# A two-block transformer-like kernel: later convolution tiles, FFNs that open on three outputs, and an earlier second half of a values' projection

## The chip, the cores and the metric

The kernel runs on one core of one Trainium2 chip. The metric is the device time of one execution in microseconds (us); lower is better. The core has TensorE (PE, matrix products into PSUM; its weight loads are listed as PEld), VectorE (DVE), ScalarE (ACT), GpSimd (POOL) and SyncE (SP), which issues the DMAs. Each engine executes its own list of instructions in order.

## The reference

All data are float32, with 512 tokens and a width of 1024. The first block is a hybrid layer: a gated causal depthwise convolution of 31 taps over 1024 channels, a state-space recurrence (S5) over 32 groups with 64 complex states, gates and an output projection. The second block is a stack of two layers, each with two SwiGLU feed-forward networks (FFNs) around a mixer; the first mixer is a short convolution beside an RWKV recurrence, the second a latent attention with 8 heads.

```python
# first block
proj = rms_norm(x) @ w_in                     # ca, cb, z_c, u_s, z_s, g_c, g_s
cu = causal_depthwise_conv(ca * sigmoid(cb))  # 31 taps
cu = silu(layer_norm(cu))
conv_out = (cu * silu(z_c)) @ w_conv_out
y = gelu(s5(u_s)); y = y * sigmoid(y @ w_glu + b_glu)
ssm_out = (y * silu(z_s)) @ w_ssm_out
x = x + rms_norm((sigmoid(g_c) * conv_out + sigmoid(g_s) * ssm_out) @ w_out)
# second block, for layer 0 (even mixer) and layer 1 (odd mixer, attention)
x = x + 0.5 * swiglu(rmsnorm(x)); x = x + mixer(rmsnorm(x)); x = x + 0.5 * swiglu(rmsnorm(x))
```

## The kernel before

**Layout and products.** The activations lie transposed, channels on partitions and 512 tokens along the row, in 8 tiles of 128 channels (`P.x`). A float32 product is made of three products in a reduced format (`mm3`, L248 to L250): the high part of the weights with the high and the low part of the data, and the low part of the weights with the high part of the data. `wload` (L235 to L237) brings 1024 weight columns by a DMA from SP into `raw` (2 buffers), casts them on ACT to `wh` and makes the remainder `wl` on DVE, each of them in 3 buffers. A projection of two outputs (`proj`) is 48 products of 128x128 by 128x512 and needs two such loads.

**Order.** The program is traced in the order of the code. A planner then makes each engine's list: it goes by priority (normally the order of the code), by free buffers and by times that it estimates itself. `tc.issue_after(ins)` keeps what is traced in its block behind `ins` on the same engine. Buffers of one tag are given out in turn.

**First block.** `block1` follows two hand-written orders, `ORDER_A` and `ORDER_B`. A letter is a step, a digit its number. `p` and `P` are projections whose gated product feeds the convolution: `p` (0, 3, 5, 7) leaves a tile `cu`, `P` (1, 2, 4, 6) leaves split tiles `cph`/`cpl`. `t` (`toeplitz`, L730 on) convolves channels of a `P` tile on PE with 96 products of 256 columns and four weight loads. `c` (`conv_`) convolves channels of a `p` tile with 31 instructions: tiles 0 and 3 on POOL (L765, with ACT's products), tiles 5 and 7 on DVE (L767, L770). Class `c` has its priority lowered by 20000, so that it fills gaps. `u` projects the S5 inputs and writes them to DRAM, `s` and `z` project gates (`zs`, `zc`). `T` makes S5's tables (L366 to L490, mainly DVE), `R` the rotation tables (`s5_rot`, L507 to L512, one chain of DVE instructions). `Q` and `K` are the two halves of `s5_pre` for a quarter of the groups (POOL outer products; then PE transposes and products and 16 small DMAs). `q`, `r`, `x`, `w` are the four parts of `s5_main` for a quarter: input products (L583), rotation and scan (L588 to L594), rotation back (L597 to L603), output products (L608, L609). `q`, `r`, `x`, `w` and `K` are kept behind the last PE product that was traced before them (`P.last_mm`). The convolution tiles on POOL are kept behind `P.last_gp` and those on DVE behind `P.last_dve`; `P.last_dve` is set in `s5_rot` (L512). In `ORDER_B`, `y` and `G` finish the S5 branch, `g` projects the output gates, `L` is the layer norm over all eight convolution tiles (it begins with L847 on `sacc`, the sum that POOL makes at L778 and L780), `S` and `C` are the two output projections. The output tiles of `z` lie in pools that are opened after those of S5 are closed.

**FFN.** `ffn` runs four times. Each of two halves makes 11 pairs (gate, up), each pair from one load of 2048 columns, and then 8 outputs of the down projection. The first FFN gets `cols=HALVES` and opens otherwise: gate 0, up 0 and gate 1 are made together, tile of data by tile of data, so that each new tile of data feeds three outputs. The other three begin with all of gate 0, then up 0. Inputs `xh`, `xl` come tile by tile from the stage before (L270, L271). The banks of PSUM are given out anew at each stage.

**Odd mixer.** `odd` makes key parts for all heads (`kall`), half of the values (`vproj(0)`, 24 products, L1889 to L1891, with evacuations L1893 and L1894), then keys and queries for pairs of heads (`kpair`, `qpair`). `kpair` reads rows of `nd` back from DRAM as broadcasts, multiplies (L1828) and splits. `qpair` makes 27 products, a rotation (L1755 on the result of L1855) and row sums (L1869). The second half of the values, `vproj(1)`, comes after the second pair's keys and queries, in two banks.

Of the kernel before, what the change touches and what calls it, by code (L numbers as in the profile page):

```python
# [296 lines left out]
def ffn(P, L, j, nxt, out=None, cols=()):  # L297
# [4 lines left out]
    with tc.tile_pool(name=f"f{L}{j}", bufs=2) as ph, tc.tile_pool(name=f"m{L}{j}", bufs=1) as mp:  # L302
# [4 lines left out]
        first = []  # L307
        if cols:
            w0, w1 = P.wload(gu[0], 2048), P.wload(gu[1], 1024)
            pss = [P.ps() for _ in range(4)]  # L310
            for s in cols:
                for k in range(8):
                    for ps, (h, l), o in ((pss[0], w0, 0), (pss[1], w0, 1024), (pss[2], w1, 0)):
                        P.mm3(ps[:, s], h, l, o + 128 * k, [P.xh[k][:, s]], [P.xl[k][:, s]], k == 0, k == 7)
            h, l = P.wload(gu[1][:, 1024:], 1024)
            P.mm3(pss[3], h, l, 0, P.xh, P.xl)
            first = [pss[0:2], pss[2:4]]
# [176 lines left out]
def s5_rot(P, tb):  # L494
# [5 lines left out]
    for i in range(6):  # L500
        m = 1 << i
        n = min(32, 512 // m)
        for g0 in range(0, 32, n):
            g = slice(g0, g0 + n)
            cq, sq = (a[:, g].unsqueeze(2).to_broadcast([128, n, m]) for a in tb["rot"][i])
            A, B = (x[:, 0:n * m].rearrange("p (g k) -> p g k", g=n) for x in (ta, tb_))
            V.tensor_tensor(out=A, in0=c[:, g, 0:m], in1=cq, op=ALU.mult)  # L507
            V.tensor_tensor(out=B, in0=s[:, g, 0:m], in1=sq, op=ALU.mult)
            V.tensor_tensor(out=c[:, g, m:2 * m], in0=A, in1=B, op=ALU.subtract)
            V.tensor_tensor(out=A, in0=s[:, g, 0:m], in1=cq, op=ALU.mult)  # L510
            V.tensor_tensor(out=B, in0=c[:, g, 0:m], in1=sq, op=ALU.mult)
            P.last_dve = V.tensor_tensor(out=s[:, g, m:2 * m], in0=A, in1=B, op=ALU.add)  # L512
# [50 lines left out]
def s5_main(P, tb, q, u_dram, y_dram):  # L563
# [39 lines left out]
    V.tensor_tensor(out=sh[:, :, 1:64], in0=st3[:, :, 0:63], in1=vr3[:, :, 0:63], op=ALU.subtract)  # L603
# [354 lines left out]
def proj_first(P, src, xT, sqx):  # L958
# [33 lines left out]
    for a in range(2):  # L992
# [6 lines left out]
ORDER_A = ("p0 P1 p3 t1 u0 u1 T Q0 P2 R0 K0 t2 Q1 c0 q0 K1 s0 r0 P4 x0 q1 Q2 s1 w0 r1 K2 p5 c3 x1 q2 Q3 t4 w1 r2 K3 P6 c5 "  # L999
           "x2 q3 t6 w2 r3 p7 x3 w3 c7")  # L1000
ORDER_B = "z0 z1 z2 z3 y0 g0 g1 g2 y1 y2 y3 g3 G L g4 g5 g6 S0 g7 S1 C0 C1 C2 C3 C4 C5 C6 C7"
# [652 lines left out]
def odd(P, nxt):  # L1654
# [14 lines left out]
    with ExitStack() as ctx:  # L1669
# [304 lines left out]

        K, Q = kpair(0), qpair(0, "all")
        for p in range(4):
# [4 lines left out]
            if p == 0:  # L1981
                vproj(1, "mm")
                S.put(*kvh, *kvl)
# [54 lines left out]
```

## Time and profile before

| | us |
|---|---|
| median of three runs | 2653.73 |
| lowest and highest run | 2647.78, 2653.99 |
| the profiled execution, own time | 2650.77 |
| span of the profiled execution | 2649.0 |
| PE busy | 2512.6 |
| DVE busy | 1474.5 |
| ACT busy | 925.5 |
| POOL busy | 484.2 |

The span runs from the first to the last instruction; the execution's own time is 1.8 us longer. PE is busy for 95% of the span, and the work that PE has to do is the same in each version of an order, so the difference between span and busy time, 136.4 us, is what an order can win, besides time in which PE ran at the lower of its two clocks. The profile gives the granted clock as a share of full speed (1.00 is 2.4 GHz, 0.50 is 1.2 GHz). By time the stages are: first block to about 576 us, first FFN to 937, even mixer to 1319, second FFN to 1680, third to 2040, odd mixer to 2278, last FFN to the end.

### The profile page before, as it was taken

How to read it: one execution, taken by the hardware profiler on the slowest of the kernel's cores; microseconds unless marked ns; L12 is line 12 of the kernel's file. 1: busy time of each engine (PE TensorE's matmuls, PEld its weight loads, DVE VectorE, ACT ScalarE, POOL GpSimd, SP SyncE). 2: the span in 40 equal slices, each digit the busy share in tenths (PEclk: the TensorE clock that was granted, in tenths of full speed). 3: DMA queues.
4: the chain of work that ended last, by engine and by line, in shares of the span. 5: the costliest groups of instructions: out<-in, count | busy, mean ns of one | idle time of the engine just before them, and what ended most of it. 6: DMA issues, size and time to landing. Idle time of an engine off the chain costs nothing.

```text
span 2649.0 us, 31923 instructions
## 1 busy us (share of the span) xinstructions
PE 2512.6 (95%) x12724; PEld 2052.6 (77%) x12724; DVE 1474.5 (56%) x1978; ACT 925.5 (35%) x1322; POOL 484.2 (18%) x332
## 2 busy tenths in 40 slices
PE   8687899999999998999899999999999889999999
PEld 7566788878888876787588888888888677788887
DVE  7888868455344469643754344543444766543443
ACT  5253436243222333222332233322223565422221
POOL 2499602020000164331100000100001231100000
PEclk9798899999999998998999999999999989999999
DMA  5222332313232332314132322322324412222323
GB/s 169 80 85 75 92 111 89 127 66 110 87 105 99 113 129 59 74 49 132 41 100 88 107 96 90 102 98 92 105 86 138 113 62 72 70 97 85 106 93 98
DMA packets 116294, 250.94 MB, mean 95 GB/s; under 512 B 44112, under 2 KB 53072, under 8 KB 116144
## 3 DMA queue, kind: packets, MB, share of 16 engines
q1 hardware_dynamic: 116000, 248.68, 29.7%
q8 instruction: 100, 1.64, 0.3%
q14 instruction: 50, 0.41, 0.0%
q10 hardware_dynamic: 144, 0.22, 0.0%
HBM read 234.30 MB, written 13.37 MB: 93 GB/s over the span
## 4 chain that ended last, share of the span: by engine, by line
PE 78%; DVE 9%; POOL 3%; issue 2%; DMA 2%; ACT 2%; SPq 0%; DVEq 0%; ACTq 0%; POOLq 0%
PE bank L248 24%; PE bank L249 24%; PE bank L250 24%; POOL xa L765 1%; DVE wl L237 1%; DMA s<-nd 1%; PE bank L1913 1%; DVE xa L770 1%; PE bank L1270 1%; POOL acc L265 1%; PE bank L1333 0%; ACT wh L236 0%; PE bank L1346 0%; DVE xl L271 0%; PE bank L1406 0%
## 5 line engine op out<-in xcount | busy, mean ns | idle before, releaser
L248 PE MATMUL bank<-xh,wh 128*128 128x512 f32 (+1 forms) x2152 | 836.7, 391 | 13.6 <-ACT xh L977 5.8
L236 ACT CAST wh<-raw 128x1024 fp32r<-128x1024 f32 x448 | 433.3, 968 | 1187.2 <-PE bank L249 852.5
L249 PE MATMUL bank<-xl,wh 128*128 128x512 f32 (+1 forms) x2152 | 838.0, 390 | 4.3 <-DVE xl L947 2.7
L250 PE MATMUL bank<-xh,wl 128*128 128x512 f32 (+1 forms) x2152 | 836.3, 389 | 2.7 <-DVE wl L237 2.7
L237 DVE TENSOR_TENSOR wl<-raw,wh 128x1024 fp32r<-128x1024 f32 (+2 forms) x414 | 482.7, 1166 | 331.8 <-ACT wh L236 329.3
L248 PEld LDWEIGHTS bank<-xh,wh 128*128 128x128 f32 x2152 | 406.8, 190 | 103.1 <-ACT xh L977 6.5
L249 PEld LDWEIGHTS bank<-xl,wh 128*128 128x128 f32 x2152 | 407.9, 190 | 92.1 <-DVE xl L978 4.6
L250 PEld LDWEIGHTS bank<-xh,wl 128*128 128x128 f32 x2152 | 407.8, 189 | 87.7 <-DVE wl L237 3.6
L265 POOL TENSOR_TENSOR acc<-acc,sq 128x512 f32<-128x512 f32 x54 | 90.1, 1669 | 1298.2 <-ACT sq L264 1291.6
L249 PE MATMUL bank<-ml,wh 128*128 128x512 f32 x704 | 273.9, 389 | 0.0
L250 PE MATMUL bank<-mh,wl 128*128 128x512 f32 x704 | 273.9, 389 | 0.0
L248 PE MATMUL bank<-mh,wh 128*128 128x512 f32 x704 | 272.6, 389 | 0.0
L332 DVE TENSOR_TENSOR up<-bank,rs 128x512 f32<-128x512 f32 x88 | 60.8, 691 | 271.5 <-PE bank L250 271.4
L328 DVE TENSOR_TENSOR gp<-bank,rs 128x512 f32<-128x512 f32 x88 | 60.8, 691 | 174.9 <-PE bank L250 174.7
L250 PEld LDWEIGHTS bank<-mh,wl 128*128 128x128 f32 x704 | 132.2, 188 | 27.6
L249 PEld LDWEIGHTS bank<-ml,wh 128*128 128x128 f32 x704 | 132.2, 188 | 27.4
L248 PEld LDWEIGHTS bank<-mh,wh 128*128 128x128 f32 x704 | 132.2, 188 | 27.3
L237 POOL TENSOR_TENSOR wl<-raw,wh 128x1024 fp32r<-128x1024 f32 x34 | 82.9, 2440 | 139.7 <-ACT wh L236 112.7
L765 POOL TENSOR_TENSOR xa<-xa,cw 128x512 f32<-128x512 f32 x60 | 98.0, 1635 | 10.7 <-ACT cw L764 8.1
L340 DVE SCALAR_TENSOR_TENSOR xa<-bank,xa 128x512 f32<-128x512 f32 x64 | 44.3, 692 | 79.5 <-PE bank L250 79.5
L254 ACT CAST mh<-m 128x512 fp32r<-128x512 f32 x88 | 55.1, 626 | 58.5 <-DVE m L334 58.5
L743 PE MATMUL bank<-cph,wh 128*128 128x256 f32 x128 | 41.0, 320 | 32.2 <-ACT cph L726 32.2
(654 smaller groups left out, 2927.8 us busy)
## 6 DMA issues: line engine op xcount, KB each, us to landing
raw<-in_ffn_gu_dram SPq DMA_DIRECT2D x176, 512.0 KB, 3.5
raw<-in_ffn_dn_dram SPq DMA_DIRECT2D x64, 512.0 KB, 3.5
raw<-in_w_in_dram SPq DMA_DIRECT2D x46, 512.0 KB, 3.5
raw<-in_even_in_dram SPq DMA_DIRECT2D x26, 512.0 KB, 3.5
raw<-in_ffn_dn_dram SPq DMA_DIRECT2D x64, 192.0 KB, 2.3
raw<-in_conv_dram SPq DMA_DIRECT2D x16, 512.0 KB, 3.8
xa<-in_xT_dram SPq DMA_DIRECT2D x16, 256.0 KB, 4.1
raw<-in_w_co_dram SPq DMA_DIRECT2D x8, 512.0 KB, 3.3
```

Of the source, the lines that this page charges most:

```text
L236: nc.scalar.copy(h[:, :m], raw[:, :m])
L237: self.wlo.tensor_tensor(out=l[:, :m], in0=raw[:, :m], in1=h[:, :m].bitcast(F32), op=ALU.subtract)
L248: self.nc.tensor.matmul(ps, h[i][:, s], xh[k], start=a, stop=False)
L249: self.nc.tensor.matmul(ps, h[i][:, s], xl[k], start=False, stop=False)
L250: last = self.nc.tensor.matmul(ps, l[i][:, s], xh[k], start=False, stop=b)
L254: self.nc.scalar.copy(hi, src)
L265: nc.gpsimd.tensor_tensor(out=acc, in0=acc, in1=sq, op=ALU.add)
L328: nc.vector.tensor_tensor(out=gp, in0=pg, in1=rs, op=ALU.mult)
L332: nc.vector.tensor_tensor(out=up, in0=pu, in1=rs, op=ALU.mult)
L340: nc.vector.scalar_tensor_tensor(out=P.x[o], in0=ps, scalar=0.5, in1=P.x[o], op0=ALU.mult, op1=ALU.add)
L743: nc.tensor.matmul(d, h[:, o], xh, start=a, stop=False)
L765: GP.tensor_tensor(out=y, in0=y, in1=w, op=ALU.add)
```

## The change

The change has three parts. In `ffn` the opening on three outputs becomes the only one; the three FFNs that had the plain opening take it with whole rows (`slice(0, T)`). In the first block `ORDER_A` is rearranged: step `P2` comes ahead of `u0`, `s0` ahead of `K0`, `P4`, `t4`, `s1`, `P6`, `t6` and `p7` each move forward by one place or more; `c5` and `c7` leave `ORDER_A` and stand behind `z0` in `ORDER_B`; `P.last_dve` is now the last DVE instruction of a step `x` (L603), so that both DVE convolution tiles stay behind step `x3`. In `odd`, `vproj(1)` stands ahead of the first pair's keys and queries and takes its banks from the large group.

```diff
--- before.py
+++ after.py
@@ -294,7 +294,7 @@
 HALVES = (slice(0, 256), slice(256, 512))
 
 
-def ffn(P, L, j, nxt, out=None, cols=()):
+def ffn(P, L, j, nxt, out=None, cols=(slice(0, T),)):
     nc, tc = P.nc, P.tc
     gu, dn = P.ap["ffn_gu"][L * 2 + j], P.ap["ffn_dn"][L * 2 + j]
     rs = P.rs
@@ -304,17 +304,15 @@
         mh = [mp.tile([128, T], R, name=f"mh{i}") for i in range(11)]
         ml = [mp.tile([128, T], R, name=f"ml{i}") for i in range(11)]
         acc = None
-        first = []
-        if cols:
-            w0, w1 = P.wload(gu[0], 2048), P.wload(gu[1], 1024)
-            pss = [P.ps() for _ in range(4)]
-            for s in cols:
-                for k in range(8):
-                    for ps, (h, l), o in ((pss[0], w0, 0), (pss[1], w0, 1024), (pss[2], w1, 0)):
-                        P.mm3(ps[:, s], h, l, o + 128 * k, [P.xh[k][:, s]], [P.xl[k][:, s]], k == 0, k == 7)
-            h, l = P.wload(gu[1][:, 1024:], 1024)
-            P.mm3(pss[3], h, l, 0, P.xh, P.xl)
-            first = [pss[0:2], pss[2:4]]
+        w0, w1 = P.wload(gu[0], 2048), P.wload(gu[1], 1024)
+        pss = [P.ps() for _ in range(4)]
+        for s in cols:
+            for k in range(8):
+                for ps, (h, l), o in ((pss[0], w0, 0), (pss[1], w0, 1024), (pss[2], w1, 0)):
+                    P.mm3(ps[:, s], h, l, o + 128 * k, [P.xh[k][:, s]], [P.xl[k][:, s]], k == 0, k == 7)
+        h, l = P.wload(gu[1][:, 1024:], 1024)
+        P.mm3(pss[3], h, l, 0, P.xh, P.xl)
+        first = [pss[0:2], pss[2:4]]
         for hh in range(2):
             for f in range(11):
                 if first:
@@ -509,7 +507,7 @@
             V.tensor_tensor(out=c[:, g, m:2 * m], in0=A, in1=B, op=ALU.subtract)
             V.tensor_tensor(out=A, in0=s[:, g, 0:m], in1=cq, op=ALU.mult)
             V.tensor_tensor(out=B, in0=c[:, g, 0:m], in1=sq, op=ALU.mult)
-            P.last_dve = V.tensor_tensor(out=s[:, g, m:2 * m], in0=A, in1=B, op=ALU.add)
+            V.tensor_tensor(out=s[:, g, m:2 * m], in0=A, in1=B, op=ALU.add)
     tb["cs"] = c, s
 
 
@@ -600,7 +598,7 @@
     st3, p23, vr3 = (a.rearrange("p (g k) -> p g k", g=8) for a in (st, p2, vr))
     V.tensor_tensor(out=vr3[:, :, 0:63], in0=p23[:, :, 0:63], in1=s[:, :, 0:63], op=ALU.mult)
     V.tensor_tensor(out=st3[:, :, 0:63], in0=st3[:, :, 0:63], in1=c[:, :, 0:63], op=ALU.mult)
-    V.tensor_tensor(out=sh[:, :, 1:64], in0=st3[:, :, 0:63], in1=vr3[:, :, 0:63], op=ALU.subtract)
+    P.last_dve = V.tensor_tensor(out=sh[:, :, 1:64], in0=st3[:, :, 0:63], in1=vr3[:, :, 0:63], op=ALU.subtract)
     yield
     py = P.side("py")
     for g in range(8):
@@ -996,9 +994,9 @@
 
 FIRST = (("w", 0, slice(0, 256)), ("x", 0, None), ("w", 0, slice(256, 1024)), ("x", 1, None), ("x", 2, None),
          ("w", 1, slice(0, 512)), ("x", 3, None), ("w", 1, slice(512, 1024)), ("x", 4, None), ("x", 5, None), ("x", 6, None), ("x", 7, None))
-ORDER_A = ("p0 P1 p3 t1 u0 u1 T Q0 P2 R0 K0 t2 Q1 c0 q0 K1 s0 r0 P4 x0 q1 Q2 s1 w0 r1 K2 p5 c3 x1 q2 Q3 t4 w1 r2 K3 P6 c5 "
-           "x2 q3 t6 w2 r3 p7 x3 w3 c7")
-ORDER_B = "z0 z1 z2 z3 y0 g0 g1 g2 y1 y2 y3 g3 G L g4 g5 g6 S0 g7 S1 C0 C1 C2 C3 C4 C5 C6 C7"
+ORDER_A = ("p0 P1 p3 t1 P2 u0 u1 T Q0 t2 R0 s0 K0 P4 Q1 c0 q0 K1 t4 r0 s1 x0 q1 Q2 p5 w0 r1 K2 P6 c3 x1 q2 Q3 t6 w1 r2 K3 p7 "
+           "x2 q3 w2 r3 x3 w3")
+ORDER_B = "z0 c5 c7 z1 z2 z3 y0 g0 g1 g2 y1 y2 y3 g3 G L g4 g5 g6 S0 g7 S1 C0 C1 C2 C3 C4 C5 C6 C7"
 B1_CLASS = {"c": "C", "t": "V", "R": "T", "T": "T", "Q": "Q", "K": "Q", "q": "S", "r": "S", "x": "S", "w": "S", "y": "S", "G": "S", "L": "L"}
 B1_PRIO = {"A": 0, "T": 0, "Q": 0, "S": 0, "C": 20000, "V": 0, "L": 0, "Z": 50000}
 CU_BUFS = 4
@@ -1972,15 +1970,14 @@
         TS(out=qe, in0=qe, scalar1=1e-6, scalar2=None, op0=ALU.mult)
         S.put(cqs)
 
+        vproj(1, "all")
+        S.put(*kvh, *kvl)
         K, Q = kpair(0), qpair(0, "all")
         for p in range(4):
             Kn = Qn = None
             if p < 3:
                 prio("N")
                 Kn, Qn = kpair(p + 1), qpair(p + 1)
-            if p == 0:
-                vproj(1, "mm")
-                S.put(*kvh, *kvl)
             if p == 2:
                 prio("O")
                 xload((4, 5, 6, 7, 0, 1, 2, 3))
```

## Rows read from the trace of the kernel before

**Rows 1.** The page's busy time by engine: share of the span, instructions.

```profile
PE 2512.6 (95%) x12724; PEld 2052.6 (77%) x12724; DVE 1474.5 (56%) x1978; ACT 925.5 (35%) x1322; POOL 484.2 (18%) x332
```

**Rows 2.** Stretches: length; busy PE, PEld, DVE, ACT, POOL; clock; DMA share, GB/s.

```profile
57.00:320.00 263.00, 203.01 (x1065) 169.57 (x1065) 217.92 (x250) 104.02 (x152) 195.96 (x134) 0.86 0.27 82
217.00:285.00 68.00, 44.65 (x247) 37.49 (x246) 67.32 (x57) 28.65 (x43) 57.78 (x35) 0.75 0.22 61
362.00:410.00 48.00, 48.00 (x213) 39.78 (x212) 20.56 (x24) 16.31 (x22) 0.00 (x0) 1.00 0.29 99
600.00:700.00 100.00, 100.00 (x441) 82.47 (x440) 52.18 (x64) 33.91 (x43) 0.00 (x0) 1.00 0.29 94
2100.00:2200.00 100.00, 75.78 (x373) 60.58 (x374) 68.79 (x153) 58.85 (x118) 33.43 (x24) 0.86 0.32 93
```

**Rows 3.** PE's waits, whole span: total us, times, longest.

```profile
PE bank L743 <- ACT cph L726: 32.2, 2, 18.6
PE bank L1755 <- ACT s L1855: 13.2, 1, 13.2
```

**Rows 4.** Timeline of PE, first block: start, length, instruction, [idle before <- releaser].

```profile
108.40 0.58 PE L743 MATMUL bank<-cph,wh 128*128 128x256 f32 x1 [18.61 <-ACT cph L726]
...
275.15 0.58 PE L743 MATMUL bank<-cph,wh 128*128 128x256 f32 x1 [13.62 <-ACT cph L726]
...
315.91 0.29 PE L609 MATMUL bank<-sh,w 128*128 128x64 f32 x1 [0.40 <-DVE sh L603]
...
409.82 0.59 PE L847 MATMUL bank<-sacc,ones 128*128 128x512 f32 x1
...
476.81 0.39 PE L248 MATMUL bank<-cah,wh 128*128 128x512 f32 x1
```

**Rows 5.** Timeline of DVE around step T, 73 to 109 us.

```profile
73.50 1.10 DVE L785 TENSOR_TENSOR u<-bank,rsl 128x512 f32<-128x512 f32 x1 [3.29 <-PE bank L250]
...
79.98 0.09 DVE L406 MEMSET pr<- 128x32 f32 x1
...
101.94 0.68 DVE L699 TENSOR_TENSOR vb<-bank,rsl 128x512 f32<-128x512 f32 x1
...
108.38 0.69 DVE L727 TENSOR_TENSOR cpl<-cp,cph 128x512 fp32r<-128x512 f32 x1 [1.43 <-ACT cph L726]
```

**Rows 6.** DVE's groups by line: two rows of 217 to 315 us, one of 315 to 362.

```profile
L770 DVE SCALAR_TENSOR_TENSOR xa<-cu,hcw,xa 128x512 f32<-128x512 f32 x30 | 39.7, 1323 | 0.6
L237 DVE TENSOR_TENSOR wl<-raw,wh 128x1024 fp32r<-128x1024 f32 x12 | 24.6, 2051 | 8.4 <-ACT wh L236 8.4
...
L770 DVE SCALAR_TENSOR_TENSOR xa<-cu,hcw,xa 128x512 f32<-128x512 f32 x30 | 22.5, 749 | 0.5
```

**Rows 7.** Timeline of POOL: its last convolution instructions, and the last sum.

```profile
303.06 4.03 POOL L765 TENSOR_TENSOR xa<-xa,cw 128x512 f32<-128x512 f32 x3
...
360.43 1.29 POOL L780 TENSOR_TENSOR sacc<-sacc,xa 128x512 f32<-128x512 f32 x1 [45.81 <-DVE xa L770]
```

**Rows 8.** Timelines of PE and ACT in the odd mixer.

```profile
2120.64 1.22 PE L1755 MATMUL bank<-s,perm 128*128 128x512 f32 x1 [13.21 <-ACT s L1855]
...
2135.09 0.80 PE L1889 MATMUL bank<-wh,s 128*128 128x512 f32 x1
...
2119.91 0.68 ACT L1855 ACTIVATE s<-bank,vec 128x512 f32<-128x512 f32 x1
...
2138.88 0.69 ACT L1893 ACTIVATE xh<-bank,scol 128x512 fp32r<-128x512 f32 x1 [1.09 <-PE bank L1891]
```

**Rows 9.** Timelines of PE and DVE where FFNs open.

```profile
2282.66 0.80 PE L248 MATMUL bank<-xh,wh 128*128 128x512 f32 x1 [3.92 <-DVE xa L1952]
...
1319.72 0.47 PE L248 MATMUL bank<-xh,wh 128*128 128x512 f32 x1 [0.56 <-DVE xa L1532]
...
592.79 0.50 PE L248 MATMUL bank<-xh,wh 128*128 128x512 f32 x1 [0.30 <-ACT wh L236]
...
2281.93 0.68 DVE L1952 TENSOR_TENSOR xa<-xa,bank 128x512 f32<-128x512 f32 x1
```

## The prediction

> **What bounds the kernel now.** I read first the page's busy times [rows 1]: PE works 2512.6 of 2649.0 us, so 136.4 us of idle PE is all that an order can give, plus what PE loses at its lower clock. A table of stretches then shows where the idle time is [rows 2]. In an FFN (600 to 700 us) PE is busy throughout, at full clock: 441 products in 100 us, 0.227 us each, which is the price of a product below. From 57 to 320 us, in the first block, PE is busy for 203.0 of 263 us, at 0.86 of full clock: 60.0 us idle. From 2100 to 2200 us, in the odd mixer, it is busy for 75.8 of 100 us. The list of PE's waits [rows 3] names the causes: 32.2 us in two waits of a toeplitz step for its `cph` tile and 13.2 us in one wait of a query's rotation; a fourth, 3.92 us, stands where the last FFN opens [rows 9]. All lie in the three places that the change touches.
>
> In the first block the timeline [rows 4] has the two toeplitz waits: t2 at 108.40 (18.61 us) and the last one, t6, at 275.15 (13.62 us). Both tiles were late on DVE, not on PE. For t2 the evacuation of P2 (L699) begins at 101.94, inside the S5 tables, although DVE had stood idle between the evacuations of u before (3.29 us ahead of the one at 73.50) [rows 5]. For t6 the place is 217 to 285 us, where DVE is busy for 67.3 of 68 us and POOL for 57.8 [rows 2]: 30 of the 31 instructions of c5 take 39.7 us there [rows 6], between S5's steps, the weights' low parts and P6.
>
> **Part 1, the first block.** I count from step u on; the PE work in it doesn't change. Step by step:
>
> - t2. P2 is now projected ahead of u, so its DVE work falls where DVE was idle, and t2 has its data when u ends. The wait of 18.61 us [rows 4] goes.
> - What that costs. P2's 48 products are 48 x 0.227 = 10.9 us by which u, and with it the S5 tables, come later: in the trace the tables start right behind the last u (79.98) [rows 5]. Part of that comes back, since P2's own DVE work, which now stands between tables and rotation chain, leaves that place. It begins with `vb` at 101.94 (0.68 us) and ends with `cpl` at 108.38 (0.69 us), which waited 1.43 us for ACT [rows 5]; table instructions stand between, so I count only P2's: `vb`, `ca` and `cpl` at 0.68 us, `cp` in four quarters at 1.7 us in all, and that wait, 5.2 us. S5 starts 10.9 - 5.2 = 5.7 us later. I charge it in full as new idle time of PE: +5.7. The bounds are 0 (s0, P4 and t4 now stand there to fill PE) and 10.9.
> - t6. Its wait followed from c5 [rows 6]. c5 leaves DVE's crowded stretch (39.7 us) and P6 moves up by a round of S5. The wait of 13.62 us goes [rows 4].
> - PE's clock. Both waits were followed by slow products: the first of t2 and of t6 took 0.58 us [rows 4]. 57 to 320 us ran at 0.86 [rows 2]. For a loss of half the speed over about 5 us after each wait I take 2 x 2.5 = 5 us back, an estimate from these rows; bounds 0 and 10.
> - The rest of the idle time, 60.0 - 32.2 = 27.8 us, I leave as it is: single waits of 0.4 to 5 us for S5 steps, weights and DMAs. If DVE's relief ends these as well, the gain is larger; half of them, 14 us, enters the low end.
> - The tail. Behind p7 there now stand x2, q3, w2, r3, x3, w3 with no projection between. Only z0 and z1 can fill, and their four outputs wait in PSUM for S5's memory: 96 x 0.227 = 21.8 us of cover. No row shows such a tail; the nearest rows are t6's start at 275.15 and w3's at 315.91 [rows 4]: 40.8 us that hold t6 and p7 beside S5's steps, so 40.8 - 2 x 10.9 = 19 us for the steps alone (t6's 96 products of 256 columns have the columns of 48 of 512). That is less than the cover; I take 4 us, for a step that waits before z's weights are there, bounds 0 and 20.
> - c5 and c7, late. Both follow x3, 62 instructions. Without POOL one takes 0.749 us, with it 1.323 [rows 6]. x3 should end near 285 us, and POOL's last convolution instruction comes at 303 to 307 [rows 7], so for some 22 us they run beside POOL, and the weights' low parts wait among them (2.05 us each [rows 6]). From 217 to 285, PE was idle for 68 - 44.65 = 23.4 us, without t6's wait 9.7 us, or 14%: of 22 us that makes 3, and I take 4; bounds 0 and 11 (half of the stretch).
> - What hides the convolutions after that: all eight tiles are needed by the layer norm's L847, at 409.82, and its result by the first output product at 476.81 [rows 4]. Now the last sum is at 360.43 [rows 7], 49 us early, and DVE from 362 to 410 has 27.4 us free [rows 2]; c5 costs 31 x 0.749 = 23.2 us there. So I cost it at nothing. If that cover goes, each us is one of PE's.
>
> The sum is -18.6 + 5.7 - 13.6 - 5 + 4 + 4 = -23.5 us. As a check on DVE: it is busy for 217.9 us from 57 to 320 [rows 2]; without c5's 39.7 and with the same 45 us of gaps, S5 would end some 35 to 40 us earlier, so DVE allows the sum.
>
> The Trainium skill (page "SBUF — State Buffer", section "Who interferes with whom") says that a DVE instruction with two SBUF inputs and a GpSimd instruction that reads SBUF exclude each other for their whole length. The two means of L770 agree with it. By this rule alone c5 and c7 gain wherever they run clear of POOL, which is what I counted, and it speaks against the change for the 22 us in which they don't.
>
> **Part 2, the odd mixer.** PE ends the first queries at 2107.4 (2120.64 less the 13.21 us of idle time) and waits until 2120.64 for the rotation, whose input ACT makes at 2119.91 behind the keys' splits [rows 8]. vproj(1) moves from 2135.09 into this gap: 24 x 0.227 = 5.4 us. Its load now goes ahead of the queries' loads on SP and takes a weight buffer; the queries' weights then come after the first outputs of the projection before, with vproj(0) and vproj(1) to cover them, so nothing. On ACT and DVE its four evacuations (about 0.7 us each) go to a time when ACT waits for DMAs. Where it was, ACT took the first evacuation at 2138.88, right ahead of the first softmax [rows 8], so that chain moves up as well. But the 13.2 - 5.4 = 7.8 us left of the gap still slow PE's clock, and the heads behind lose a filler. Bounds: -6.5 and +3; I take -4.
>
> **Part 3, the FFNs.** The opening on three outputs exists in the first FFN; its fourth output waits three times for weights, 0.76 us in all, 0.30 in its first row [rows 9]. Each of three FFNs pays this, 2.3 us together. The second gains what it waits now (0.56 us [rows 9]), the third nothing, as PE shows no wait where it opens. The last waits 3.92 us for the evacuation L1952, which ends at 2282.6, and its first product takes 0.80 us, against 0.50 at the first FFN's wait [rows 9]: by this a loss of 0.2 to 0.3 us for each of some ten slow products, an estimate of 2.4 us. More outputs for each new tile of data could fill that time, but the last tiles' evacuation still comes at 2281.93. I take half of 3.92 + 2.4, -3.1. Sum: 2.3 - 0.6 - 3.1 = -1.4; bounds -6 and +3.
>
> **In all** -23.5 - 4 - 1.4 = -28.9 us on the profiled execution's 2650.8: 2621.9. The median was 3.0 us above it, so 2625.
>
> **Rivals.**
> *A. S5's latency is the bound.* Steps q to w are held behind the projections and their own round trips through DMA, PE, ACT and DVE; with fewer projections in a round PE only waits elsewhere. Then the two toeplitz waits come back as waits in the tail, S5's later start eats the relief of c5, and parts 2 and 3 are left: about 2648, within 0.3%. For it: the 27.8 us of small waits are mostly S5's. Against it: c5 stands directly ahead of S5's steps on a full DVE.
> *B. S5 keeps its length from tables to w3 and starts 10.9 us later, and the odd mixer gives nothing.* Place: 90 to 330 us; price: +10.9, with the fill of z lost (the tail's 4 us taken again) and the FFNs' 2.3: about 2670. It decides as soon as DVE isn't what delays S5's steps. Against it: the same row of 67.3 in 68 us.
> *C. The relief goes on.* Half of the small waits end too, and the tail is covered: -28.9 - 14 - 8 = -51, about 2603.
>
> **How the numbers follow.** A change under 0.3% (8 us) can't be told from none here. Forecast, 2604 to 2644: 0.65. C and more: 0.12. A: 0.12. B: 0.11. So faster 0.77, same 0.12, slower 0.11. The range of 8 in 10 takes the forecast's bounds, most of C and a part of A: 2600 to 2652.
>
> **What would show it.** Right: t2 begins at about 90 us without a wait; no toeplitz step waits over 5 us; w3 ends at 280 to 300; idle PE from 57 to w3 falls to about 35 us; L847 without a wait; the odd gap at about 8 us. Wrong: waits of PE for S5 steps (L597, L609, L583) that sum to 15 us or more behind p7, L743 still waiting for `cph`, PE waiting for `wl` behind L770 after x3, or L847 late with idle PE before it.

## The result, and the profile after

The changed kernel takes 2633.59 us (median of four runs, 2630.64 to 2637.35), against 2652.46 for the kernel before in the same comparison: a ratio of 0.9937, 95% interval 0.9916 to 0.9958. That is faster by 16.7 us with an interval of 11 to 22 us, or by 18.9 us as a difference of the medians; the prediction was 2625, 28.7 us below the median it started from, so some six tenths to two thirds of the forecast gain came. The profiled execution of the changed kernel took 2636.32 us, one of the longer ones, 14.45 us less than the profiled execution of before (2650.77).

Lines from L309 on carry numbers that are two lower than in the listing, since part 3 shortens `ffn`: t2's products are L741 to L743, the evacuation of `vb` is L697, the rotation chain L505 to L510, the convolution instruction on DVE L768, the layer norm's sum L845.

The page's busy times, which answer to [rows 1]:

```profile
PE 2517.7 (96%) x12724; PEld 2053.9 (78%) x12724; DVE 1458.4 (55%) x1978; ACT 924.2 (35%) x1322; POOL 476.7 (18%) x332
```

Two stretches of the changed kernel; columns as in [rows 2], with the number of instructions in brackets behind each busy time. The second one is moved by the 10 us by which the odd mixer begins earlier:

```profile
57.00:320.00 263.00, 217.93 (x1133) 180.88 (x1132) 193.72 (x236) 110.71 (x161) 185.05 (x133) 0.88 0.31 91
...
2090.00:2190.00 100.00, 81.35 (x402) 65.49 (x402) 73.14 (x156) 61.56 (x121) 37.35 (x26) 0.89 0.33 96
```

From 57 to 320 us PE is idle for 263 - 217.9 = 45.1 us where it was 60.0. The list of PE's waits over the span (total, times, longest) shows that the two waits of [rows 3] went or shrank, and what came; its three longest:

```profile
PE bank L551 <- ACT vs L583: 13.6, 1, 13.6
...
PE bank L741 <- ACT cph L724: 6.5, 1, 6.5
...
PE bank L551 <- ACT m L543: 5.4, 1, 5.4
```

The first line is new and nearly as long as the one that the change removed. The timeline of PE in the first block, which answers to [rows 4]:

```profile
89.57 0.28 PE L741 MATMUL bank<-cph,wh 128*128 128x256 f32 x1
...
117.66 0.79 PE L250 MATMUL bank<-xh,wl 128*128 128x512 f32 x1 [4.01 <-DVE wl L237]
...
138.16 1.23 PE L551 MATMUL bank<-w,s5bb 128*16 128x128 f32 x5 [5.39 <-ACT m L543]
...
158.54 0.80 PE L551 MATMUL bank<-w,s5bb 128*16 128x128 f32 x3 [13.63 <-ACT vs L583]
...
238.22 0.58 PE L741 MATMUL bank<-cph,wh 128*128 128x256 f32 x1 [6.55 <-ACT cph L724]
...
314.98 0.77 PE L248 MATMUL bank<-xh,wh 128*128 128x512 f32 x1 [3.47 <-DVE zc L797]
...
394.92 1.02 PE L845 MATMUL bank<-sacc,ones 128*128 128x512 f32 x2
```

t2 starts at 89.57 without a wait, 18.8 us earlier than in [rows 4]. But before PE has done the S5 products that follow it, it waits 4.01 + 5.39 + 13.63 = 23.0 us in three other places. t6 waits 6.55 us instead of 13.62, and at 315 us there is a wait for the evacuation of z0. L845 does not wait.

To say where the time went, I compare both timelines at seven points that have the same work behind them. The table gives, for the profiled execution of each kernel, how much earlier (-) or later (+) than in the profiled execution of before PE reaches each point. It is worked out from the timelines of PE; the points are the first product of squares ahead of the first FFN (L934, L932 where part 3 is in), the last product of each of the first three FFNs, of both mixers, and of the whole kernel.

| kernel | first FFN begins | first FFN | even mixer | second FFN | third FFN | odd mixer | end |
|---|---|---|---|---|---|---|---|
| changed kernel | -14.65 | -12.31 | -12.10 | -10.66 | -10.04 | -13.46 | -14.44 |
| e1, first block's part alone | -14.44 | -13.14 | -12.22 | -12.21 | -12.21 | -14.69 | -14.87 |
| e2, values' projection alone | +0.33 | +1.27 | +0.80 | +0.81 | +0.81 | -6.01 | -5.85 |
| e3, FFN openings alone | +0.96 | +0.91 | +5.55 | +6.92 | +7.55 | +7.36 | +6.38 |
| e5, P2 ahead of u alone | +4.20 | +5.56 | +6.11 | +6.10 | +6.10 | +6.37 | +6.21 |
| e6, late c5 and c7 alone | -16.65 | -15.31 | -10.97 | -10.94 | -10.94 | -12.24 | -12.31 |
| e7, P4 ahead of R0 | -15.21 | -15.26 | -7.08 | -5.70 | -5.08 | -13.33 | -13.09 |
| e8, P2 put back | -19.85 | -18.55 | -18.21 | -16.80 | -16.17 | -21.90 | -21.69 |
| e9, convolutions behind z0 | -20.21 | -18.88 | -12.85 | -11.43 | -10.80 | -16.15 | -15.96 |
| e10, e8 and e9 together | -19.62 | -19.67 | -20.67 | -19.26 | -18.61 | -26.90 | -26.62 |
| e11, e10 with plain openings | -21.25 | -21.31 | -22.50 | -22.50 | -22.51 | -28.34 | -28.23 |
| e14, e11 with s0 ahead of P2 | -25.00 | -24.06 | -21.30 | -21.33 | -21.33 | -28.39 | -29.77 |

In the changed kernel the first block gives 14.65 us, the odd mixer 3.42 (from -10.04 to -13.46), and the last FFN 0.98; the first three FFNs take back 2.34, 1.44 and 0.62. The even mixer, which the change does not touch, moves by up to 8 us from one execution to another (the last section shows where). So the end of a profile is read here only with the timed ratio beside it, and the steps are judged at the points nearest to them. Kernels with the same first block differ at the first FFN's beginning by up to 1.6 us (e10 and e11; the kernel before, e2 and e3 by up to 1.0), so differences of that size are not read.

### The profile page after: what moved, and what is told of

Its sections match the earlier page's. It is cut to its first block, busy times and chain, and to the rows that moved or that the text cites. A ratio compares the mean times of both kernels' runs of the same rounds, so it can differ in the third digit from the quotient of the medians.

```text
span 2634.6 us, 31923 instructions
## 1 busy us (share of the span) xinstructions
PE 2517.7 (96%) x12724; PEld 2053.9 (78%) x12724; DVE 1458.4 (55%) x1978; ACT 924.2 (35%) x1322; POOL 476.7 (18%) x332
## 4 chain that ended last, share of the span: by engine, by line
PE 81%; DVE 9%; POOL 3%; issue 2%; DMA 2%; ACT 2%; SPq 1%; DVEq 0%; ACTq 0%; POOLq 0%
PE bank L248 24%; PE bank L250 24%; PE bank L249 24%; POOL xa L763 2%; DVE wl L237 1%; POOL acc L265 1%; PE bank L1911 1%; DMA raw<-in_w_in_dram 1%; PE bank L1268 1%; ACT wh L236 0%; PE bank L1331 0%; DMA s<-nd 0%; SPq L557 0%; PE bank L1344 0%; PE bank L1404 0%
## 5 line engine op out<-in xcount | busy, mean ns | idle before, releaser
L249 PEld LDWEIGHTS bank<-ml,wh 128*128 128x128 f32 x704 | 132.2, 188 | 27.4
L250 PEld LDWEIGHTS bank<-mh,wl 128*128 128x128 f32 x704 | 132.2, 188 | 27.4
L248 PEld LDWEIGHTS bank<-mh,wh 128*128 128x128 f32 x704 | 132.2, 188 | 27.4
L332 DVE TENSOR_TENSOR m<-up,sg 128x512 f32<-128x512 f32 x88 | 60.9, 692 | 10.9 <-ACT sg L328 2.3
```

The source lines that it names most:

```text
L248: self.nc.tensor.matmul(ps, h[i][:, s], xh[k], start=a, stop=False)
L249: self.nc.tensor.matmul(ps, h[i][:, s], xl[k], start=False, stop=False)
L250: last = self.nc.tensor.matmul(ps, l[i][:, s], xh[k], start=False, stop=b)
L332: nc.vector.tensor_tensor(out=m, in0=up, in1=sg, op=ALU.mult)
```

## The parts one by one

**e1, the first block's part alone.** The two orders, L512, L603 as in the changed kernel; `ffn` and `odd` as before.

> The first block's part alone; the FFNs and the odd mixer as before. Theory: the 14.7 us by which the first FFN starts earlier in the changed kernel all come from this part, and the planner's new place for one square at the first FFN's opening gives 2.3 us of it back, so the time is 12 to 15 us below before (about 2638 to 2641), with the 13.6 us wait of L551 in the trace as in the changed kernel. Rival: part of the gain needs the other parts (the planner's lists differ), and the time is under 8 us below before.

Measured: 2638.78 us, ratio 0.9950 (0.9936 to 0.9964), 12 us below the 2650.93 of before on that chip; first FFN 14.44 us earlier. The theory holds for the time and for the wait (13.6 us here too); the first FFN's opening gives back 1.30 us, not 2.3.

**e2, the values' projection alone.**

```diff
+        vproj(1, "all")
+        S.put(*kvh, *kvl)
         K, Q = kpair(0), qpair(0, "all")
...
-            if p == 0:
-                vproj(1, "mm")
-                S.put(*kvh, *kvl)
```

> Only the second half of the values' projection is moved. Theory: from the third FFN's end to the last FFN's first product the changed kernel took 3.4 us less, and that is this part's own: 2 to 5 us below before, with the wait for the first queries' rotation split into waits of 4 to 5 us for the values' low part and 1 to 2 us. Rival: the gain came with the shift of the stage against its DMAs, and alone it gives 0 to 1 us.

Measured: 2644.94 us, ratio 0.9975 (0.9967 to 0.9984): 4 to 9 us faster, somewhat more than expected; the odd mixer is 6.82 us shorter in the profile (0.81 to -6.01). The rotation's wait of 13.21 us in [rows 8] became these, here in the changed kernel:

```profile
2105.26 0.50 PE L248 MATMUL bank<-s,wh 128*128 128x512 f32 x1 [4.38 <-DVE xl L1892]
2110.95 1.72 PE L1867 MATMUL bank<-slide,s 128*128 128x1 f32 x14 [0.65 <-POOL s L1864]
2113.77 0.79 PE L248 MATMUL bank<-s,wh 128*128 128x512 f32 x1 [1.11 <-DVE s L1755]
```

They sum to 6.1 us. The rotation (L1753) does not wait any more, and the product that waits now waits for the low part of the values' own evacuation.

**e3, the FFN openings alone.**

> Only the opening on three outputs in three more FFNs. My prediction had 1.4 us less. Theory from the trace of the changed kernel: the second FFN loses 1.4 us, the third 0.6 us, each at its fourth output, and the last gains 1 us, so 0 to 2 us above before. Rival: the last FFN gains 3 us or more as predicted, and the time is 1 us or more below before.

Measured: 2652.08 us, ratio 1.0008 (0.9999 to 1.0017). In the profile the second FFN costs 1.37 us more and the third 0.63, as in every kernel here that has the openings; the last gains 0.98 in this kernel and in the changed one, but loses 0.2 to 0.3 in e7 to e10, which open alike, and gains 1.38 in e14, which has the plain opening. So the profiles show a loss from the openings and no gain, and the timing does not tell part 3 from no change. Most of the +6.38 at the end of this profile stands in the even mixer. The second FFN's loss is at the fourth output, as the timeline of PE in the changed kernel shows:

```profile
1307.63 0.47 PE L248 MATMUL bank<-xh,wh 128*128 128x512 f32 x1 [0.56 <-DVE xa L1530]
...
1327.16 0.50 PE L250 MATMUL bank<-xh,wl 128*128 128x512 f32 x1 [0.80 <-DVE wl L237]
...
2269.20 0.50 PE L248 MATMUL bank<-xh,wh 128*128 128x512 f32 x1 [3.92 <-DVE xa L1950]
```

Both waits of [rows 9] are as long as before. The 0.56 us stand in front of the second FFN's first product, where the number of outputs makes no difference. The 3.92 us of the last FFN stand behind two products of its opening (at 2264.55 and 2264.89 us here, at 2278.01 and 2278.34 before) and end with the odd mixer's last evacuation; they are 3.91 to 3.93 us in every kernel of the table, so the products of two more outputs filled none of it. Why they did not is not shown.

## Where the first block's gain comes from

**e7, P4 ahead of the rotation chain.** My first reading of the new 13.63 us wait was the chain of releasers in the changed kernel. ACT's and then DVE's timeline:

```profile
157.29 0.63 ACT L698 ACTIVATE vb<-vb 128x512 f32<-128x512 f32 x1 [14.20 <-DVE vb L697]
157.82 0.57 ACT L583 COPY vs<-bank 128x512 f32<-128x512 f32 x1
```

```profile
90.83 0.09 DVE L404 MEMSET pr<- 128x32 f32 x1
...
120.28 0.21 DVE L505 TENSOR_TENSOR ra<-rc,rc 128x32 f32<-128x32 f32 x1 [1.07 <-ACT rc L478]
...
155.97 0.68 DVE L509 TENSOR_TENSOR rb<-rc,rs 128x512 f32<-128x512 f32 x1
156.57 0.68 DVE L697 TENSOR_TENSOR vb<-bank,rsl 128x512 f32<-128x512 f32 x1
```

PE waits for a copy on ACT; ACT stands for 14.20 us at the activation of P4's `vb`; and DVE makes that `vb` only behind most of the rotation chain. So P4 should go ahead of the chain:

```diff
-... P2 u0 u1 T Q0 t2 R0 s0 K0 P4 Q1 c0 ...
+... P2 u0 u1 T Q0 t2 P4 R0 s0 K0 Q1 c0 ...
```

> The changed kernel with P4 placed ahead of R0 and Q1 behind K0, so that P4's evacuation (L697) has a better rank on DVE than the rotation chain (L505 to L510). Theory: the new 13.6 us wait of L551 comes from ACT, whose next instruction was the sigmoid of P4's vb, which DVE evacuated only behind the rotation chain; with P4's vb inside the chain the wait falls under 4 us and the time is 8 to 14 us below the changed kernel, about 2620 to 2625. Rival: S5 starts later because P2 goes ahead of the S5 inputs, and PE only waits elsewhere between 110 and 180 us; then the time stays within 3 us of the changed kernel's 2633.

Measured: 2637.96 us (2624.95 to 2643.64), ratio 0.9939 (0.9918 to 0.9960); first FFN 15.21 us earlier, where the changed kernel has 14.65. The theory fell, and the rival stands. L551's long wait is gone, and PE waits for the same length elsewhere:

```profile
145.09 0.58 PE L741 MATMUL bank<-cph,wh 128*128 128x256 f32 x1 [13.21 <-ACT cph L724]
150.30 0.58 PE L742 MATMUL bank<-cpl,wh 128*128 128x256 f32 x1 [4.63 <-DVE cpl L725]
...
315.60 0.77 PE L248 MATMUL bank<-xh,wh 128*128 128x512 f32 x1 [11.82 <-DVE zc L797]
```

Now t4 waits for P4's tile, and the wait for z0's evacuation is 11.82 us where it was 3.47. The releaser was named rightly, but ending its wait gave nothing. That DVE, busy with tables and rotation, holds up whatever PE is given to do there is how I read the two lists; no run took that work off DVE. The next two runs ask what P2's move and c5's move are worth by themselves.

**e5, P2 ahead of u alone**, an edit of the kernel before:

```diff
-ORDER_A = ("p0 P1 p3 t1 u0 u1 T Q0 P2 R0 K0 t2 ...
+ORDER_A = ("p0 P1 p3 t1 P2 u0 u1 T Q0 R0 K0 t2 ...
```

> The kernel before with one step moved: P2 ahead of u0. By my prediction's terms: t2's wait of 18.6 us goes, S5 starts 5.7 us later, some 2.5 us of clock come back, so 15 us below before (about 2636). Theory now: PE has no other work between the S5 inputs and the end of the rotation chain on DVE (L505 to L510 in the changed kernel), the chain starts some 11 us later, and the wait comes back at other steps; the first FFN starts 5 us earlier to 5 us later than before, and the sum of PE's idle time between 57 and 320 us stays within 6 us of its 60.0.

Measured: 2656.17 us, ratio 1.0023 (1.0007 to 1.0039): slower, where the prediction's terms make it 15 us faster. The first FFN begins 4.20 us later. The wait of t2 is gone; in its place the list of PE's waits from 57 to 330 us has these, first the S5 step x, behind its scan on DVE:

```profile
PE bank L597 <- DVE st L594: 18.0, 2, 16.9
PE bank L544 <- ACT kt L555: 7.7, 1, 7.7
PE bank L583 <- ACT m L545: 6.2, 1, 6.2
```

One expectation was missed: the idle time from 57 to 320 us is 49.3 us (213.66 busy), 10.7 less than the 60.0 of before. The clock there is no higher (0.85, with 0.86 in [rows 2]), only eleven more products are done by 320 us, and from 320 to 402 us PE is idle for another 4.4 us (77.65 busy of 82.00), where it had been busy throughout. What became of the time is counted under e8, up to the first FFN.

**e6, late convolutions alone**, again from the kernel before:

```diff
-... w1 r2 K3 P6 c5 x2 q3 t6 w2 r3 p7 x3 w3 c7"
+... w1 r2 K3 P6 x2 q3 t6 w2 r3 p7 x3 w3"
-ORDER_B = "z0 z1 ...
+ORDER_B = "z0 c5 c7 z1 ...
```

together with `P.last_dve` at L603.

> The kernel before with c5 and c7 alone moved behind step x3 (with the line that holds them there); the rest of the order as it was. By my prediction's terms: t6's wait of 13.6 us goes with 2.5 us of clock, and 4 us come back beside POOL: some 8 to 12 us below before (2639 to 2643). Theory now: nearly the whole gain of the first block is this move, 10 to 15 us below before. Rival: S5's own round trips set the time, the wait moves from t6 to S5's steps, and the gain is under 4 us.

Measured: 2636.20 us, ratio 0.9941 (0.9925 to 0.9958); first FFN 16.65 us earlier, more than in the whole change. The stretch from 217 to 285 us, against the second row of [rows 2], then the last instruction of step x3 on DVE, here and in the kernel before:

```profile
217.00:285.00 68.00, 57.63 (x363) 51.43 (x362) 40.35 (x33) 39.20 (x58) 61.29 (x42) 0.89 0.33 96
```

```profile
297.34 1.76 DVE L603 TENSOR_TENSOR sh<-st,vr 128x504 f32<-128x504 f32 x1
```

```profile
315.10 0.67 DVE L603 TENSOR_TENSOR sh<-st,vr 128x504 f32<-128x504 f32 x1
```

DVE is busy for 40.4 us instead of 67.3, PE idle for 10.4 instead of 23.4, and the clock stands at 0.89 instead of 0.75. Step x3 ends at 299.1 us where it ended at 315.8, 16.7 us earlier, and the first FFN starts as much earlier. The 18.6 us wait of t2 is still there, untouched, and t6 still waits 8.65 us of 13.62. Up to the first FFN PE's idle time is 13.2 us shorter than before (47.4 of 60.6), so some 8 us of the gain are smaller waits; PE's busy time is 3.5 us shorter.

**e8, the changed kernel with P2 put back:**

```diff
-... t1 P2 u0 u1 T Q0 t2 R0 ...
+... t1 u0 u1 T Q0 P2 t2 R0 ...
```

> The changed kernel with P2 put back behind u1, T and Q0, all else as changed. By my prediction's terms the wait of t2 returns and the kernel is some 13 to 15 us slower than the changed one (about 2647). Theory now: S5 starts 11 us earlier, and the place of P2 is worth 5 us at most either way (2628 to 2638).

Measured: 2632.70 us, ratio 0.9932 (0.9910 to 0.9954), and the first FFN 5.20 us earlier than in the changed kernel. t2 waits again, as long as ever:

```profile
108.53 0.58 PE L741 MATMUL bank<-cph,wh 128*128 128x256 f32 x1 [18.49 <-ACT cph L724]
```

By time e8 and the changed kernel are not told apart (0.9937 there); the 5.20 us are those of the profiles.

Why a wait of 18 us is worth nothing shows when the way to the first FFN is split into PE's idle and busy time. The products on it are the same (2142 to 2148 in the records). The stretches from 57 us to the first FFN's beginning, columns as in [rows 2]: the kernel before and e5, then e8 and the changed kernel:

```profile
57.00:559.81 502.81, 442.25 (x2142) 367.82 (x2142) 364.71 (x436) 206.72 (x293) 218.87 (x148) 0.93 0.30 96
57.00:564.01 507.01, 452.74 (x2143) 374.11 (x2143) 371.37 (x436) 207.35 (x293) 218.74 (x148) 0.92 0.30 95
```

```profile
57.00:539.96 482.96, 435.46 (x2146) 363.24 (x2145) 347.30 (x436) 208.34 (x294) 209.01 (x148) 0.95 0.32 100
57.00:545.16 488.16, 442.29 (x2143) 366.70 (x2142) 347.75 (x436) 205.89 (x293) 210.09 (x148) 0.94 0.31 99
```

| P2 ahead of u | wait of t2 that goes | PE's idle time | PE's busy time | first FFN begins |
|---|---|---|---|---|
| e5 against before | -18.6 | -6.3 | +10.5 | +4.2 |
| changed kernel against e8 | -18.5 | -1.6 | +6.8 | +5.2 |

Two things happen. Most of the wait comes back at other steps, so the idle time falls by far less than 18 us. And PE takes longer over the same products, because more of them run at 1.2 GHz: by the trace's clock records, 54 us of PE's busy time from 57 to 320 us in e5 against 37 before, and 36 in the changed kernel against 24 in e8. In the kernel before, most of the first low stretch fell into t2's wait, when PE had nothing to do (from 80 to 110 us the clock is 0.73 and PE busy for 11.2 of 30 us). In the changed kernel shorter waits follow each other and the clock is low while PE works between them (from 137 to 167 us it is 0.50, PE busy for 13.0 of 30 us). Profiles of one and the same first block (before, e2 and e3; the changed kernel and e1; e10 and e11) differ by up to 1.9 us in busy time and 1.0 us in idle time, so the busy times of both pairs and the idle time of the first are clear of that.

The end of S5's chain does not explain the two pairs. Step x3 ends at 309.1 us in e5, 6.7 us earlier than before, though the first FFN starts later; and it ends at 304.1 in e8 and at 304.3 in the changed kernel, though 5.20 us lie between them at the first FFN.

The runs also split the first block's 14.65 us: the late convolutions -16.65 (e6), the moves of s0, P4, t4, s1, P6, t6 and p7 together -3.20 (from e6 to e8), P2 +5.20. The middle term is no more than twice the spread, and its moves were not tried one by one.

**e14, another filler for the same wait.** In e11 below, s0 goes ahead of P2; unlike P2's move, this leaves the S5 tables where they are.

```diff
-... u0 u1 T Q0 P2 t2 R0 s0 K0 P4 ...
+... u0 u1 T Q0 s0 P2 t2 R0 K0 P4 ...
```

> The same (with plain openings), and s0 placed ahead of P2, so that PE has another projection to do while DVE makes the S5 tables, and the tables still start right behind u1. By my prediction's reading of t2's wait the gain would be 8 to 11 us, since the 18.5 us wait of L743 at 108 us loses 10.9 us to useful work. Theory now: projections are only exchanged; what PE does not wait for here it waits for behind the rotation chain, and P2's evacuation comes later into that chain, so the first FFN starts within 4 us of the kernel without this edit.

Measured: 2622.15 us, ratio 0.9888 (0.9872 to 0.9905), against 2621.43 and 0.9891 (0.9874 to 0.9909) for e11: no difference. The first FFN starts 3.75 us earlier than in e11, of the 10.9 us of useful work that went into the gap. t2's wait has grown even so:

```profile
124.22 0.58 PE L743 MATMUL bank<-cph,wh 128*128 128x256 f32 x1 [23.34 <-ACT cph L726]
```

## The tail, and a version that is faster than both

**e9, the convolutions behind z0's evacuation.** In the changed kernel DVE takes eleven instructions of c5 and c7 and one low part between the end of x3 and the first L797, and PE waits 3.47 us for that L797. Its timeline:

```profile
302.70 1.62 DVE L601 TENSOR_TENSOR sh<-st,vr 128x504 f32<-128x504 f32 x1
304.25 2.89 DVE L765 TENSOR_SCALAR xa<-cu,hcw,vec 128x512 f32<-128x512 f32 x2
307.06 2.07 DVE L768 SCALAR_TENSOR_TENSOR xa<-cu,hcw,xa 128x512 f32<-128x512 f32 x3
309.05 1.21 DVE L237 TENSOR_TENSOR wl<-raw,wh 128x1024 fp32r<-128x1024 f32 x1
310.18 4.05 DVE L768 SCALAR_TENSOR_TENSOR xa<-cu,hcw,xa 128x512 f32<-128x512 f32 x6
314.16 1.87 DVE L797 TENSOR_TENSOR zc<-bank,rsl 128x512 f32<-128x512 f32 x3
```

```diff
-                TT(out=z, in0=ps, in1=rs, op=ALU.mult)
+                P.last_dve = TT(out=z, in0=ps, in1=rs, op=ALU.mult)
```

> The changed kernel with c5 and c7 held behind the second evacuation of z0 (L797) instead of behind x3. Theory: in the changed kernel some ten instructions of c5 and c7 stand ahead of the first L797 on DVE, which is what the 3.5 us wait of PE at 315 us comes from; with them behind it the wait goes and the first FFN starts 2 to 4 us earlier than in the changed kernel, with L847 still not waiting (its sum was made 7 us early). Rival: L797 waits for memory that S5's last steps and their DMAs hold, the wait stays near 3 us, and L847 becomes late by a few us.

Measured: 2629.29 us, ratio 0.9917 (0.9898 to 0.9937); first FFN 5.56 us earlier than in the changed kernel, more than expected. The first evacuation of z0 now runs at

```profile
309.52 1.89 DVE L797 TENSOR_TENSOR zc<-bank,rsl 128x512 f32<-128x512 f32 x3 [2.94 <-issue]
```

which is 4.64 us earlier, and PE's list of waits no longer has one for `zc`. By time the intervals of e9 and of the changed kernel overlap. L845 stands later in PE's list and does not wait.

**e10, e8 and e9 together.**

> The changed kernel with both edits that helped: P2 back behind Q0, and c5 and c7 held behind the second L797. Theory: each removed a different delay (the S5 tables' start 11 us late; ten convolution instructions ahead of z0's evacuation), so the gains at the first FFN's start add up in part: 22 to 26 us earlier than before, against 14.7 in the changed kernel, and 2625 to 2630 in time. Rival: with P2 back the wait for z0's evacuation is short already, the two gains are one, and the time is that of either alone, 2629 to 2633.

Measured: 2625.57 us, ratio 0.9905 (0.9890 to 0.9920). The time is where the theory had it, but the first FFN begins 19.6 us earlier than before (21.25 in e11, whose first block is the same), not 22 to 26: the first block gains no more than with either edit alone. The rest stands in the odd mixer, 8.29 us in this profile where it was 3.42 in the changed kernel's, and in an even mixer that ran a little shorter. So for the first block the rival is right: the two gains are one, and with c5 and c7 behind z0's evacuation the place of P2 makes no difference that these profiles resolve.

**e11, and with the plain openings** for the last three FFNs.

> The same with the three later FFNs opened as before the change. Theory: the second FFN's opening on three outputs costs 1.4 us and the third's 0.6 us, the last one's gives 1.0 or nothing, so this is 1 to 2 us faster than with the openings. Rival: the last opening's gain balances them, and the two are within 0.5 us.

Measured: 2621.43 us, ratio 0.9891 (0.9874 to 0.9909). The second and third FFN lose nothing now (-22.50 to -22.51). The intervals of e10 and e11 overlap; the profile shows 1.4 + 0.6 us for the openings. By its median this version is 30.5 us faster than before on the same chip, and by the ratios, whose intervals do not overlap, 12 us faster than the changed kernel. It keeps c5 and c7 late and the moves of s0, P4, t4, s1, P6, t6 and p7, and the values' projection; it drops P2's move and the openings.

## The prediction, point by point

- **The direction and the range** were right; the size of the forecast gain was not. By the profiles, 28.9 us were forecast and 14.45 came; by the medians, 28.7 and 18.9. That the time lies in the range is in part luck: P2's move was counted as 15.4 us of gain (-18.6 + 5.7 - 2.5) and cost 5.2, while the late convolutions gave 8.5 us more than was counted and the other moves, which the sum left out, 3.2.
- **t2, -18.6.** This is the step that failed: "The wait of 18.61 us goes" was true and was no gain. The sum counted the whole wait, as if none would come in its place; the idle time fell by 6.3 us (e5) and 1.6 us (e8 to the changed kernel), and PE's busy time grew by more than that. P2's move measured +4.2 us by itself (e5) and cost 5.2 us in the changed kernel (e8), and e14's filler gave 3.75 us of 10.9. Rival A said that PE would only wait elsewhere, but put both toeplitz waits under it; that holds for t2 alone. Its cause, S5's latency, is not shown: x3's end does not move with the first FFN.
- **PE's clock, -5 for both waits.** Nothing came back: PE's busy time up to the first FFN is 442.29 us in the changed kernel and 442.25 before. For t2 the sign was wrong, since the low clock beside a long wait costs little while PE has nothing to do; in e6, which moves only c5 and c7, it is 438.78.
- **S5 later, +5.7.** The mechanism was right and the size was not quite: the tables start 10.85 us later (90.83 against 79.98 in [rows 5]), but the 5.2 us that P2 was to leave free did not come back. The rotation chain starts at 120.28 (108.99 before). In the 29 us ahead of it DVE is as full as before (28.2 us busy of 29.4, and 27.4 of 29.0); five weights' low parts stand there instead of three, which is 2.5 of the 5.2 us. The later start did not last to S5's end: in e5 x0 ends 4.2 us later than before and x3 6.7 us earlier. This is the group in the changed kernel, 90.8 to 120.2 us, and in the kernel before, 79.9 to 108.9 us:

```profile
L237 DVE TENSOR_TENSOR wl<-raw,wh 128x1024 fp32r<-128x1024 f32 x5 | 6.1, 1216 | 0.0
```

```profile
L237 DVE TENSOR_TENSOR wl<-raw,wh 128x1024 fp32r<-128x1024 f32 x3 | 3.6, 1212 | 0.0
```

- **t6 and c5, -13.6, with 2.5 us of clock against it +4 and +4**, so -8.1 in all: measured -16.65 (e6). The place was right, the gain was undersized, and the wait that I counted is the smaller part: t6's wait falls by 5.0 us in e6 and by 7.1 in the changed kernel. What c5 delayed was S5's third round: x2 ends at 259.9 us in e6 where it ended at 275.8, the last round follows with the same length, and the first FFN comes as much earlier as x3.
- **The tail, +4, and the 22 us beside POOL, +4**: together they were the 3.47 us wait for z0, 5.6 us by e9. The size was about right, the mechanism was the order on DVE and not the mixing with POOL. Step x3 ended at 304.3 us, not near 285, when POOL's last convolution instruction had ended: of the 60 instructions L768 one took 1350 ns, beside POOL's sum at 383.4, and the others 737 to 750.
- **The cover of the late convolutions** held: L845 does not wait.
- **The odd mixer, -4**: 3.42 us in the changed kernel's profile, 6.82 in e2, 4 to 9 by e2's timing. The mechanism was right, and the gap left over is 6.1 us for 7.8 expected; by itself the part reached just beyond the lower bound of -6.5. The profiles scatter: the table's odd mixer is 3.4 to 8.3 us shorter in the kernels with this part, and from 0.3 longer to 2.5 shorter in those without it.
- **The FFNs, -1.4**: wrong in sign by the profiles. Part 3 costs 2.1 us in the changed kernel's profile (1.44 + 0.62), and nothing that the timing of e3 shows. The opening costs the second FFN about 1.4 us, not 0.76, of which the wait at the fourth output is 0.80; and the last FFN's 3.92 us wait stayed whole. What [rows 9] shows for it, and the prediction calls its first product, is the first behind the wait. The 0.98 us that the last FFN gave are fewer slow products behind that wait. They do not go with the opening: e14 has them without it, and e7 to e10 have the opening without them.
- **Not foreseen**: the first FFN, whose code is unchanged, lost 2.34 us at its opening. ACT's list there had one square more ahead of the casts of the fourth output's weights, and PE waited 1.36 us for the cast where [rows 9] has 0.30. That is some 1.1 us; e1 and e8 have the same wait and lose 1.30 there. The other 1.0 us came with a lower clock right behind it in this one execution: 0.66 from 580 to 585 us, where the same stretch of e1 has 1.00.

```profile
579.19 0.50 PE L248 MATMUL bank<-xh,wh 128*128 128x512 f32 x1 [1.36 <-ACT wh L236]
```

  The planner makes this list from its own estimates, which the new order upstream changes; that is argued, and no run was made for it.
- **The signs that the prediction named.** Right were t2 at 89.57 us without a wait, L845 without one, and the odd mixer's gap of 6.1 us. Not so: t6 still waits 6.55 us, w3 stands at 304.5 to 308.6 us and not at 280 to 300, and PE's idle time from 57 us to its end is 41.6 us, not about 35.

## What to carry to other kernels

A wait's length says how long an engine stood, not what its removal is worth: other waits can take its place, and the same products can then run at a lower clock. So compare the engine's idle and its busy time over the whole stage, and try the move by itself. Here the work that was worth moving was what crowded VectorE among S5's steps (c5's 31 instructions, moved with c7's: 16.65 us), and not the step in front of the longest wait (P2 on TensorE: 4 us the wrong way). Instructions that are allowed to be late need a hold behind the evacuations that free PSUM too, not only behind the chain that they were in the way of (e9: 5.6 us at the first FFN).

## What the hardware showed beside it

**The clock in a stretch that no edit touches.** The runs of one kernel spread over 3.5 us (e6) to 18.7 us (e7) here, and the even mixer is a place where profiles differ. Both kernels do the same work in these rows, first the changed kernel, then e7 (columns as in [rows 2]; the granted clock is the third number from the end):

```profile
1189.00:1197.00 8.00, 5.89 (x69) 5.35 (x69) 4.10 (x8) 1.63 (x2) 2.35 (x1) 0.64 1.25 240
1197.00:1205.00 8.00, 8.00 (x100) 7.82 (x98) 4.79 (x9) 0.58 (x1) 0.00 (x0) 0.50 0.25 99
1205.00:1213.00 8.00, 8.00 (x88) 6.33 (x87) 2.71 (x4) 0.36 (x1) 1.04 (x1) 0.79 0.31 95
1213.00:1221.00 8.00, 8.00 (x98) 6.38 (x95) 1.37 (x2) 2.50 (x5) 2.37 (x2) 1.00 0.29 98
```

```profile
1194.00:1202.00 8.00, 8.00 (x76) 6.66 (x76) 4.01 (x7) 0.00 (x0) 1.04 (x1) 0.50 0.46 162
...
1218.00:1226.00 8.00, 8.00 (x74) 6.35 (x74) 0.69 (x1) 2.39 (x5) 2.98 (x2) 0.50 0.07 25
1226.00:1234.00 8.00, 8.00 (x46) 5.92 (x45) 1.37 (x2) 2.68 (x4) 0.44 (x1) 0.91 0.51 173
```

After some idle time (PE busy for 5.89 of 8 us in the first row) the clock is granted at half, 1.2 GHz. In the changed kernel it is back at full speed from 1213 us on; in e7 PE is just as busy and the clock stays at 0.50 until 1226. That one stage then takes 8.18 us longer than in before (the table: -15.26 to -7.08), against 0.21 longer in the changed kernel. Why the clock comes back later in one execution than in another is open.

**DVE beside POOL.** The rotation chain on 512 columns shows what the convolution's means in [rows 6] had shown, a doubling: L508 took 0.69 us at 155.36, while POOL stood in its 15.94 us wait, and 1.48 us at 164.45, when POOL was at work again (last row):

```profile
155.36 0.69 DVE L508 TENSOR_TENSOR ra<-rsn,rc 128x512 f32<-128x512 f32 x1
...
164.45 1.48 DVE L508 TENSOR_TENSOR ra<-rsn,rc 128x512 f32<-128x512 f32 x1
...
163.82 1.56 POOL L528 TENSOR_TENSOR t<-s5bb,s5t 128x512 f32<-128x512 f32 x1 [15.94 <-PE bank L542]
```

This agrees with the rule of the Trainium skill that the prediction drew on (page "SBUF — State Buffer", section "Who interferes with whom"). What that was worth to the time of the chain, no run here measures.
